# Two middle feed-forwards with one group of raw activations and an output product of seven block products

## The chip, the cores and the metric

One core of one Trainium2 chip runs the whole program. The metric is the device time of one execution in microseconds; lower is better. Before the change three executions took 1884.76, 1885.07 and 1885.96 us (median 1885.07). The engines are TensorE (PE: matmuls; its weight loads are listed apart as PEld), the vector engine (DVE), ScalarE (ACT), GpSimd (POOL, which here issues DMAs, and does so for all DMAs that add to what lies at their destination) and SyncE (SP, which issues the other DMAs). Each engine runs its own instructions strictly in the order in which they were built into the program.

## The reference

A decoder trunk of two layers on 512 tokens of width 1024. Each layer has three sub-layers: a feed-forward, a token mixer, a feed-forward. With c the conditioning vector and nine modulation vectors per layer:

```
mod = (silu(c) @ w_ada[l] + b_ada[l]).reshape(9, 1024)      # sh1, sc1, gt1, sh2, ... gt3
hn  = rms_norm(h, g_ffn1[l]) * (1 + sc1) + sh1
h   = h + 0.5 * (1 + gt1) * swiglu(hn, w_ffn1_in[l], w_ffn1_out[l])
hn  = rms_norm(h, g_mix[l]) * (1 + sc2) + sh2
h   = h + (1 + gt2) * mixer(hn)
hn  = rms_norm(h, g_ffn2[l]) * (1 + sc3) + sh3
h   = h + 0.5 * (1 + gt3) * swiglu(hn, w_ffn2_in[l], w_ffn2_out[l])

swiglu(x) = (silu(x @ w_in[:, :2816]) * (x @ w_in[:, 2816:])) @ w_out
```

So there are four feed-forwards; the middle two are the second of layer 0 and the first of layer 1. Both take their input from one norm and hand their result to the next.

## The kernel before, in words

The residual h lies in SBUF as eight tiles of 128 features by 512 tokens; "lower" and "upper" half are tokens 0 to 255 and 256 to 511 (`lo_`, `hi_`, `HALVES`). Every product is done in three matmuls: each operand is split into a high part and the remainder (`split`, L103: a cast on ACT at L104, a subtraction on DVE at L105), and high x high, high x low and low x high are summed in PSUM. A weight block of 128 x 1024 numbers is thus loaded raw (512 KB), split into `wH` and `wL` (four buffers each), and used.

A feed-forward (`ffn`) makes 22 tiles of activations, taken as 11 pairs. In the middle feed-forwards the first two pairs are products over the whole depth of 1024 (`projector`). The other nine go through `pair_in`: the pair's gate and up columns, times the two halves of depth, times the two token halves, are done as seven block products (24 matmuls of 256 columns each) instead of eight. Their weights are four raw blocks A(g, kh) and sums of them. Two sums are made by a DMA that adds at its destination (`plus`, L408, on POOL), two by DVE (L497, L524).

Before the change the middle feed-forwards work in two groups (`GROUPS`, tiles 0 to 11 and 12 to 21). The activations of a group are split at once into `actH` and `actL` (`put`); then the output product of that group runs over eight output tiles with matmuls of 512 columns (`pieces`, L93 to L95), and each tile is added to h (`residual`, L312). The last two output tiles of the second group run in token halves (`close`), so that the next norm (`norm`: `stats`, `spread`, `apply`, `low`) of the lower half goes on beside the upper half's matmuls; from there on DVE and ACT follow the order in which the code is written (`manual_schedule`).

The modulation vectors come from dots on DVE (`ada_dot`, L168): 128 rows of `w_ada`, a DMA of 512 KB from POOL's queue for each (L182), times silu(c). In the middle feed-forwards `ada_steps` puts two or three of them beside each output tile, 36 in a feed-forward.

The last feed-forward works otherwise (`whole_k`): it keeps all activations raw in one group (`raw`, six tiles), and its output product is cut in two along output features, depth and tokens and done as seven block products of 132 matmuls of 256 columns (`out_strassen`, `plan`, matmuls at L661), in 42 units whose loads, splits and sums are prepared some units ahead. Its eight dots run as half rows, one per pair (`half_dots`). Where the code sets no order, a scheduler decides it when the program is built; `issue_after` ties single instructions.

Of the kernel before, what the change touches and what calls it, by code (L numbers as in the profile page):

```python
# [8 lines left out]
F32 = mybir.dt.float32  # L9
# [7 lines left out]
P = 128  # L17
# [18 lines left out]
GROUPS = ((0, 12), (12, 22))  # L36
RWKV_WORK, ATT_WORK, FILL_WORK = 29.8, 15.2, 129.6
# [23 lines left out]
def trunk_kernel(ctx, tc, ins, out, layers=L, phases=("ffn1", "mix", "ffn2")):  # L61
# [156 lines left out]
    def norm(l, g, ish, isc, ss):  # L218
# [18 lines left out]
        def spread(sl):  # L237

            r, pt = rstd[sl.start], psum([P, T // 2], "ps_rstd", "r0" if sl.start else "x")
# [23 lines left out]
    loads = []  # L263

# [15 lines left out]
    def projector(srcs, hn, tags, pts=None, ahead=0, ready=None):  # L280
# [8 lines left out]
        if pts is None:  # L289
            pts = [psum([P, T], "ps_mm", tag) for tag in ("mm", "mm", "r1")]  # L290
            for sl in HALVES:
                for k in range(KD):
                    for w, pt in zip(ws, pts):
                        mm3(pt[:, sl], w, k, hn[k], sl, k == 0 and sl is HALVES[0], k == KD - 1 and sl is HALVES[1])
# [77 lines left out]
    def ffn(l, w_in, w_pair, w_out, hn, im, ss, need, then, ready, first=None, late=None):  # L372
# [6 lines left out]
        with tc.tile_pool(name="act", bufs=1) as ap_:  # L379
# [3 lines left out]
            whole_k = ss is None  # L383
# [26 lines left out]
            raws_ = []  # L410

            def new_raw():
                raws_.append(ap_.tile([P, 2, 2, T], F32, name="raw", tag="raw", bufs=6))
                return raws_[-1]

            def corner(X):
                return tt(X[:, 0, hi_], X[:, 1, hi_], X[:, 0, hi_], ALU.subtract)

            def new_x(p):

                if whole_k:
                    return (new_raw() if p % 2 == 0 else raws_[-1])[:, p % 2]
# [49 lines left out]
            def put(X, sl, x, y):  # L472
                if whole_k:
                    done_ = tt(X[:, :, sl], x, y, ALU.mult)
                    return corner(X) if sl is hi_ else done_
                tt(x, x, y, ALU.mult)
# [3 lines left out]
            def pair_in(p):  # L480
# [1162 lines left out]
```

## Time and profile before

| what | value |
|---|---|
| median of three executions | 1885.07 us |
| the profiled execution | 1883.92 us |
| its span, first to last instruction | 1881.8 us |
| TensorE busy | 1853.7 us (99%) |
| DVE busy | 1462.8 us (78%) |
| ACT busy | 871.5 us (46%) |
| DMA, mean over the span | 169 GB/s |
| 2nd feed-forward, from its first projection to the next one's | 621.20 to 961.02 us |
| 3rd feed-forward | 961.02 to 1301.93 us |
| last feed-forward, pairs by block products | 1595.70 to 1767.42 us |
| last feed-forward, its output product | 1767.42 to the end |

The profile is of one execution; all stage lengths below are in its time, counted from the span's first instruction. A busy share says how much of a stretch an engine had an instruction in flight. Matmuls overlap, so their rate is read from how many start in a stretch, not from the duration of one. In a row of grouped instructions the name in front is the tile that is written.

### The profile page before, as it was taken

The numbers are of one execution on the slowest core, as the hardware profiler recorded it, in microseconds if no ns is written. First come the engines' busy times: TensorE is split into PE (matmuls) and PEld (weight loads), VectorE is DVE, ScalarE is ACT, GpSimd is POOL, SyncE is SP. The second block draws the span as 40 slices with busy tenths as digits, with TensorE's granted clock in tenths as the row PEclk, the third lists the DMA queues.
The fourth block names the chain that finished last, engine by engine and source line by source line (L and its number), as shares of the span: only waits on it lengthen the run. The fifth ranks groups of instructions, "written<-read, shape, count | busy, mean of one in ns | idle before, by whom it ended". The sixth has DMA issues, their size and how long they took to land.

```text
span 1881.8 us, 37923 instructions
## 1 busy us (share of the span) xinstructions
PE 1853.7 (99%) x15796; PEld 1733.0 (92%) x15796; DVE 1462.8 (78%) x2320; ACT 871.5 (46%) x1312; POOL 155.9 (8%) x243
## 2 busy tenths in 40 slices
PE   9999999999999999999999999999999999999999
PEld 8998899897889999899899989999878889999999
DVE  7787687858886877678787776878498768888996
ACT  4453355346432555245345524544554335555653
POOL 0101100100000010110100011110000000111120
PEclk9999999999999999999999999999999999999999
DMA  8667877521222285886817688782211315787855
GB/s 305 245 180 235 261 200 235 169 71 46 75 60 71 90 228 167 291 221 188 278 56 204 174 270 234 190 267 83 91 53 60 94 39 160 213 226 210 234 129 141
DMA packets 110028, 317.19 MB, mean 169 GB/s; under 512 B 23968, under 2 KB 29088, under 8 KB 108832
## 3 DMA queue, kind: packets, MB, share of 16 engines
q1 hardware_dynamic: 78192, 203.33, 31.6%
q0 software_dynamic: 31664, 111.43, 24.2%
q8 instruction: 124, 2.03, 0.4%
q14 instruction: 48, 0.39, 0.1%
HBM read 311.31 MB, written 3.41 MB: 167 GB/s over the span
## 4 chain that ended last, share of the span: by engine, by line
PE 83%; DVE 11%; ACT 2%; issue 2%; DMA 2%; SPq 0%; ACTq 0%; DVEq 0%
PE ps_mm L101 16%; PE ps_mm L94 8%; PE ps_mm L93 8%; PE ps_mm L95 8%; PE ps_d L467 7%; PE ps_d L469 6%; PE ps_d L468 6%; PE ps_f L469 3%; PE ps_f L467 3%; PE ps_f L468 3%; PE ps_d L661 2%; PE ps_g L469 2%; PE ps_g L467 1%; PE ps_g L468 1%; PE ps_f L661 1%
## 5 line engine op out<-in xcount | busy, mean ns | idle before, releaser
L104 ACT CAST wH<-wraw 128x1024 fp32r<-128x1024 f32 (+3 forms) x266 | 249.1, 940 | 402.0 <-PE ps_mm L94 102.2
L105 DVE TENSOR_TENSOR wL<-wraw,wH 128x1024 fp32r<-128x1024 f32 (+3 forms) x266 | 286.6, 1081 | 69.2 <-ACT wH L104 68.6
L467 PE MATMUL ps_d<-comH,wH 128*128 128x256 f32 x816 | 226.1, 277 | 1.2 <-ACT s L511 0.7
L468 PE MATMUL ps_d<-comL,wH 128*128 128x256 f32 x816 | 225.3, 276 | 0.0
L469 PE MATMUL ps_d<-comH,wL 128*128 128x256 f32 x816 | 225.2, 276 | 0.0
L93 PE MATMUL ps_mm<-actH,wH 128*128 128x512 f32 (+1 forms) x588 | 216.5, 368 | 0.0
L94 PE MATMUL ps_mm<-actL,wH 128*128 128x512 f32 (+1 forms) x588 | 216.0, 367 | 0.0
L95 PE MATMUL ps_mm<-actH,wL 128*128 128x512 f32 (+1 forms) x588 | 216.0, 367 | 0.0
L168 DVE SCALAR_TENSOR_TENSOR wada<-wada,crep 128x1024 f32<-128x1024 f32 (+1 forms) x148 | 169.4, 1162 | 48.1 <-DMA wada<-in_wadaT 47.8
L101 PE MATMUL ps_mm<-hnH,wL 128*128 128x256 f32 x976 | 199.5, 282 | 1.0 <-DVE wL L105 1.0
L101 PE MATMUL ps_mm<-hnH,wH 128*128 128x256 f32 x976 | 197.4, 282 | 0.6 <-ACT wH L104 0.3
L101 PE MATMUL ps_mm<-hnL,wH 128*128 128x256 f32 x976 | 197.2, 280 | 0.0
L104 ACT CAST wH<-sum 128x1024 fp32r<-128x1024 f32 x122 | 128.5, 1054 | 139.1 <-PE ps_d L468 66.4
L105 DVE TENSOR_TENSOR wL<-sum,wH 128x1024 fp32r<-128x1024 f32 x122 | 149.1, 1223 | 54.6 <-ACT wH L104 54.5
L101 PEld LDWEIGHTS ps_mm<-hnH,wL 128*128 128x128 f32 x976 | 149.5, 188 | 8.5 <-issue 6.6
L101 PEld LDWEIGHTS ps_mm<-hnH,wH 128*128 128x128 f32 x976 | 148.7, 188 | 8.5 <-issue 5.1
L467 PEld LDWEIGHTS ps_d<-comH,wH 128*128 128x128 f32 x816 | 153.2, 188 | 2.6 <-ACT s L511 1.7
L101 PEld LDWEIGHTS ps_mm<-hnL,wH 128*128 128x128 f32 x976 | 149.5, 188 | 5.2 <-issue 4.9
L468 PEld LDWEIGHTS ps_d<-comL,wH 128*128 128x128 f32 x816 | 153.2, 188 | 0.0
L469 PEld LDWEIGHTS ps_d<-comH,wL 128*128 128x128 f32 x816 | 153.2, 188 | 0.0
L95 PEld LDWEIGHTS ps_mm<-actH,wL 128*128 128x128 f32 x588 | 110.9, 189 | 18.3
L93 PEld LDWEIGHTS ps_mm<-actH,wH 128*128 128x128 f32 x588 | 110.9, 189 | 18.2
(474 smaller groups left out, 4716.4 us busy)
## 6 DMA issues: line engine op xcount, KB each, us to landing
wada<-in_wadaT POOLq DMA_DIRECT2D x120, 512.0 KB, 5.1
wraw<-in_wmi SPq DMA_DIRECT2D x40, 512.0 KB
wraw<-in_w2p SPq DMA_DIRECT2D x36, 512.0 KB
wraw<-in_w1p SPq DMA_DIRECT2D x32, 512.0 KB
wraw<-in_w1o SPq DMA_DIRECT2D x32, 384.0 KB
wraw<-in_w1i SPq DMA_DIRECT2D x20, 512.0 KB
wraw<-in_w1o SPq DMA_DIRECT2D x32, 320.0 KB
sum<-in_w2p SPq DMA_DIRECT2D x18, 512.0 KB
```

The source lines that it names most:

```text
L93: mm(acc, wH, xH, start=start, stop=False)
L94: mm(acc, wH, xL, start=False, stop=False)
L95: mm(acc, wL, xH, start=False, stop=stop)
L101: mm(acc[:, sl], w[a][:, k], x[b][:, sl], start=start and n == 0 and sl is HALVES[0], stop=stop and n == 2, skip_group_check=True)
L104: nc.scalar.copy(hi, src)
L105: return nc.vector.tensor_sub(lo, src, hi.bitcast(F32))
L168: stt(w, w, 1.0, crep, ALU.mult, ALU.mult, accum_out=out_)
L467: mm(pt[:, i], wH, x[k][0], start=start and i + k == 0, stop=False, skip_group_check=True)
L468: mm(pt[:, i], wH, x[k][1], start=False, stop=False, skip_group_check=True)
L469: last = mm(pt[:, i], wL, x[k][0], start=False, stop=k == 3, skip_group_check=True)
L661: mm(pt[m // 2][:, m % 2], w[:, 4 * k + m], x[:, y, k], start=start and u + k + n + m % 2 == 0, stop=u == NU - 1 and n == 2, skip_group_ch ...
```

## The change

The old `ffn` stays for the first feed-forward alone and loses its `whole_k` branches. A new function `ffn_whole` serves the other three.

- Activations of all 22 tiles stay raw in six tiles R, in one group. There is no split into `actH`/`actL`, and the output stage is `out_product`: 7 block products of 132 matmuls, in 42 units, as in the last feed-forward before. Instead of writing one block product's result into two places in h, its PSUM tile pD is copied into pG by ACT, twice.
- In `pair_in` the block A(1,1) is loaded into a buffer of its own (`third` and `crep` in turn) and stays; the sum with A(1,0), made by a DMA before, is made by DVE (L735). The remaining accumulating DMA adds A(1,0) onto A(0,0) in its one buffer `first` (L746). The two last products change places.
- The dots: 36 in each middle feed-forward, by the table `DOTS` (by pair: five in each of pairs 2 to 7, three in pairs 8 and 9; none beside the output product), eight in the last (two in each of pairs 2 to 5). Their rows are loaded into parts of R that are not yet filled: three buffers up to pair 7, one from pair 8 on.
- In the middle feed-forwards the first six block products finish the upper token half of all of h; the seventh ends the lower half of output tiles 4 to 7. Beside it the next norm's upper half is written, and the next projection starts with its upper half (`lead`). The lower half's norm follows.

Line numbers of the changed kernel that matter here: split L105/L106, dot L169, dot load L700, sums L735, L745, L772, accumulating DMA L746, block product matmul L912, h L919, norm L252/L259.

```diff
+DOTS = ((0, 0, 2, 2, 2, 2), (0, 0, 5, 5, 5, 5, 5, 5, 3, 3))
...
-            for sl in HALVES:
+            first_, second_ = lead[0]
+            lead[0] = HALVES
+            for sl in (first_, second_):
...
+    def ffn_whole(l, w_in, w_pair, w_s, hn, im, ss, need, then, ready):
...
+            R = [ap_.tile([P, 2, 2, T], F32, name="raw", tag="raw", bufs=NU) for _ in range(NU)]
+            spare = [R[-2][:, 0], R[-2][:, 1], R[-1][:, 0], R[-1][:, 1]]
...
+            crow = flat(spare[3])
...
+            def dot(behind):
+                l_, i_, k = todo.pop(0)
+                w = flat(spare[turn_[0] % 3 if behind_p[0] < 8 else 2])
+                turn_[0] += 1
+                nc.gpsimd.dma_start(w, ins["wadaT"][l_, i_, k])
...
+                with queue_behind(behind):
+                    ada_dot(mod[l_, i_][:, k : k + 1], w, crow)
...
+            def pair_in(p):
...
+                S = raw(A(1, 0), ("sum0", "sum1")[p % 2], after_="a00")
+                a11 = raw(A(1, 1), ("third", "crep")[p % 2])
+                tt(S, S, a11, ALU.add)
+                with queue_behind(order["s2"] if second_ else None):
+                    S_ = hl(S)
+                prod(pF, S_, P1, True)
+                up = half_("up")
+                taken = nc.scalar.copy(up, pF)
+                a00 = raw(A(0, 0), "first", "a00")
+                prod(pD, hl(a00), B11, True)
+                s1 = half_("s1")
+                copied = nc.scalar.copy(s1, pD)
+                tt(S, S, a00, ALU.add)
+                nc.gpsimd.dma_start(a00, A(1, 0), accum_op=ALU.add)
...
+                for f in waiting:
+                    done[0] = f()
+                waiting.clear()
+                dots(done[0])
...
+                    second = hl(S)
...
+                    middle = prod(pD, second, P2, False)
...
+                    a01 = raw(A(0, 1))
+                    right = hl(a01)
+                    prod(pG, right, B21, True)
+                gate = half_("gate")
+                mark = tt(gate, pG, s1, ALU.add)
+                act(gate, gate, AF.Silu)
+                dots(mark)
+                tt(S, S, a01, ALU.add)
...
+                prod(pF, last, B22, False)
+                mark = tt(s2, pF, s2, ALU.add)
+                act(s2, s2, AF.Silu)
+                dots(mark)
+                third = hl(a00)
+                prod(pD, third, T3, False)
+                mark = tt(up, pD, up, ALU.add)
+                dots(mark)
+                tt(X[:, :, hi_], up, s2, ALU.mult)
+                mark = corner(X)
+                dots(mark)
...
+                with tc.manual_schedule(engines=HAND):
+                    for t in range(end, len(units) - 2):
+                        prepare(t)
+                        for _ in unit(t):
+                            pass
+                        if t == end:
+                            finish(5, range(4))
+                        if t == end + 1:
+                            stats(hi_)
+                            ahead(0, raws[0])
+                        if t == end + 2:
+                            spread(hi_)
+                            ahead(1, raws[1])
+                    ahead(2, raws[2])
+                    apply(hi_, range(2))
+                    k = 2
+                    for m in unit(len(units) - 1):
+                        finish(6, (m,))
+                        apply(hi_, range(k, k + 1))
+                        k += 1
+                    stats(lo_)
+                    apply(hi_, range(k, KD))
+                    ahead(3, raws[3])
+                    spread(lo_)
+                    apply(lo_, range(KD))
+                    lead[0] = (hi_, lo_)
+                    return low_()
...
-            marks = ffn(l, ins[w + "i"], ins[w + "p"], ins[w + "o"], hn, im, nss, need, then, ready, first, late)
+            if n:
+                marks = ffn_whole(l, ins[w + "i"], ins[w + "p"], ins[w + "s"], hn, im, nss, need, then, ready)
+            else:
+                marks = ffn(l, ins[w + "i"], ins[w + "p"], ins[w + "o"], hn, im, nss, need, then, ready, first, late)
```

How this moves instructions, at three places. First DVE, inside one pair of the second feed-forward. Before, one pair's middle stretch (`sum_9912` is the sum of the pair that ends, `sum_10145` that of the next):

```order
L105 TENSOR_TENSOR wL<-wraw,wH 128x1024
L478 TENSOR_TENSOR actL<-up,actH 128x2x256
L105 TENSOR_TENSOR wL<-third,wH 128x1024
L476 TENSOR_TENSOR gate<-gate,ps_d 128x512
L105 TENSOR_TENSOR wL<-sum_9912,wH 128x1024
L478 TENSOR_TENSOR actL<-gate,actH 128x2x256
L105 TENSOR_TENSOR wL<-sum_10145,wH 128x1024
L497 TENSOR_TENSOR sum_10145<-sum_10145,first 128x1024
L521 TENSOR_TENSOR gate<-ps_g,s_9975 128x512
L105 TENSOR_TENSOR wL<-first,wH 128x1024
L530 TENSOR_TENSOR up<-ps_d,up 128x512
```

The changed kernel on DVE at the like place, from the sum at L745 on (`first` is A(0,0) at the sum and has A(1,0) added when it is split further below; the dots are the rows at L169):

```order
L745 TENSOR_TENSOR sum_9218<-sum_9218,first 128x1024
L652 TENSOR_TENSOR raw<-raw 128x256
L169 SCALAR_TENSOR_TENSOR raw,mod_2_8977<-raw 128x1024
L106 TENSOR_TENSOR wL<-crep,wH 128x1024
L106 TENSOR_TENSOR wL<-sum_9218,wH 128x1024
L106 TENSOR_TENSOR wL<-wraw,wH 128x1024
L772 TENSOR_TENSOR sum_9218<-sum_9218,wraw 128x1024
L791 TENSOR_TENSOR raw<-gate,ps_d 128x2x256
L169 SCALAR_TENSOR_TENSOR raw,mod_2_8977<-raw 128x1024
L106 TENSOR_TENSOR wL<-sum_9218,wH 128x1024
L106 TENSOR_TENSOR wL<-first,wH 128x1024
L735 TENSOR_TENSOR sum_9452<-sum_9452,crep 128x1024
```

The splits of activations are gone from the pair; dots and one more sum now stand between the weight splits, and a weight split behind a dot runs after it.

Second, POOL's queue in the same feed-forward. Before, in the pairs of group 1, it holds the accumulating DMAs alone:

```order
L408 DMA third_9376<-in_w2p 128x1024
L408 DMA sum1_9446<-in_w2p 128x1024
L408 DMA third_9609<-in_w2p 128x1024
L408 DMA sum0_9679<-in_w2p 128x1024
L408 DMA third_9842<-in_w2p 128x1024
L408 DMA sum1_9912<-in_w2p 128x1024
```

The changed kernel, over two pairs (`raw_7360` and `raw_7361` are the last two tiles of R, where the dots' rows land):

```order
L746 DMA first_8305<-in_w2p 128x1024
L700 DMA raw_7360<-in_wadaT 128x1024 x2
L700 DMA raw_7361<-in_wadaT 128x1024
L700 DMA raw_7360<-in_wadaT 128x1024 x2
L746 DMA first_8541<-in_w2p 128x1024
L700 DMA raw_7361<-in_wadaT 128x1024
L700 DMA raw_7360<-in_wadaT 128x1024 x2
L700 DMA raw_7361<-in_wadaT 128x1024
L700 DMA raw_7360<-in_wadaT 128x1024
```

One accumulating DMA a pair instead of two, and five dot loads behind each.

Third, DVE where the second feed-forward hands over. Before, beside the last output tiles' upper halves, the lower half of the norm:

```order
L234 RECIPROCAL rstd<-rstd 128x2
L105 TENSOR_TENSOR wL<-wraw,wH 128x1024
L251 SCALAR_TENSOR_TENSOR hn_t<-h_86,gmod,ps_rstd 128x256
L251 SCALAR_TENSOR_TENSOR hn_t<-h_88,gmod,ps_rstd 128x256
L258 SCALAR_TENSOR_TENSOR hnL<-hn_t,mod_0_8895,hnH 128x256
L312 SCALAR_TENSOR_TENSOR h_98<-ps_mm,cg,h_98 128x256
L251 SCALAR_TENSOR_TENSOR hn_t<-h_90,gmod,ps_rstd 128x256
L258 SCALAR_TENSOR_TENSOR hnL<-hn_t,mod_0_8895,hnH 128x256
```

Changed, beside the end of the seventh block product, the upper half of the norm and the four lower tiles of h:

```order
L106 TENSOR_TENSOR wL<-wraws,wH 128x1024
L252 SCALAR_TENSOR_TENSOR hn_t<-h_86,gmod,ps_rstd 128x256
L252 SCALAR_TENSOR_TENSOR hn_t<-h_88,gmod,ps_rstd 128x256
L259 SCALAR_TENSOR_TENSOR hnL<-hn_t,mod_0_8261,hnH 128x256
L919 SCALAR_TENSOR_TENSOR h_94<-ps_g,cg,h_94 128x256
L212 TENSOR_TENSOR ss<-ss,sq 128x256
L252 SCALAR_TENSOR_TENSOR hn_t<-h_90,gmod,ps_rstd 128x256
L259 SCALAR_TENSOR_TENSOR hnL<-hn_t,mod_0_8261,hnH 128x256
L919 SCALAR_TENSOR_TENSOR h_96<-ps_g,cg,h_96 128x256
L212 TENSOR_TENSOR ss<-ss,sq 128x256
```

Four finished tiles, each with its sum of squares, alternate with rows of the norm, where before there were two.

More of the change, by code (lines that the diff above doesn't have):

```diff
@@ L237, in spread @@
         def spread(sl):
-            r, pt = rstd[sl.start], psum([P, T // 2], "ps_rstd", "r0" if sl.start else "x")
+            r, pt = rstd[sl.start], psum([P, T // 2], "ps_rstd", "r0" if sl.start and not whole_ else "x")
             for b in range(2):
@@ L428, in ffn @@
             rows_, sums = [], {}
-            free_rows = [new_raw()[:, i] for _ in range(2) for i in range(2)] if whole_k else []
-            raws_.clear()
             def whole(n):
                 for k in (2 * n, 2 * n + 4):
-                    x = free_rows.pop(0) if whole_k else ap_.tile([P, 2, T], F32, name="x", tag="act", bufs=12)
+                    x = ap_.tile([P, 2, T], F32, name="x", tag="act", bufs=12)
                     for i in range(2):
@@ L689, in ffn, with rest @@
+                tt(up, s2, up, ALU.mult)
+                put(X, hi_, up)
+                def rest():
+                    prod(pD, hl(raw(A(1, 1))), T4, False)
+                    tt(gate, pD, gate, ALU.mult)
+                    return put(X, lo_, gate)
+                waiting.append(rest)
             turn_ = [0]
@@ L702, in ffn @@
             crep = ada_crep(ap_) if n_first == 4 else None
-            sums_ = small_.tile([P, 2, KD], F32, name="adas", tag="adas", bufs=1) if whole_k else None
-            def half_dots(after):
-                l_, i_, k = todo.pop(0)
-                ws = [sp.tile([P, T], F32, name="wada", tag="ss") for _ in range(2)]
-                for n, w in enumerate(ws):
-                    nc.gpsimd.dma_start(w, ins["wadaT"][l_, i_, k, :, n * T : n * T + T])
-                with tc.issue_after(after.ins):
-                    for n, w in enumerate(ws):
-                        ada_dot(sums_[:, n, k : k + 1], w, crep[:, n * T : n * T + T])
-                if not todo:
-                    m = mod[l_, i_] = const.tile([P, KD], F32, name=f"mod{l_}_{i_}")
-                    tt(m, sums_[:, 0], sums_[:, 1], ALU.add)
-                    tt(m, m, prm(l_, "b_ada")[:, i_ * KD : i_ * KD + KD], ALU.add)
-            for g, (j0, j1) in enumerate(((0, NF),) if whole_k else GROUPS):
+            for g, (j0, j1) in enumerate(GROUPS):
                 for p in range(j0 // 2, j1 // 2):
@@ L753, in ffn @@
                         after[0] = None
-                        if whole_k and p > n_first:
-                            crep = crep or ada_crep(ap_)
-                            half_dots(done[0])
-                if whole_k:
-                    return out_strassen(waiting.pop(), raws_)
                 flush()
@@ L1369, in normed @@
         g, im = what[p]
-        return norm(l, g, im, im + 1, ss)
+        return norm(l, g, im, im + 1, ss, n > 1 and seq[n - 1][1] != "mix")
     def begin(pool):
```

458 lines of the change are left out of this document (301 added, 157 removed).

## The prediction

> **What bounds the kernel now.** I read the page first: shares of the engines, then the chain that ended last.
>
> ```profile
> span 1881.8 us, 37923 instructions
> PE 1853.7 (99%) x15796; PEld 1733.0 (92%) x15796; DVE 1462.8 (78%) x2320; ACT 871.5 (46%) x1312; POOL 155.9 (8%) x243
> PEclk9999999999999999999999999999999999999999
> PE 83%; DVE 11%; ACT 2%; issue 2%; DMA 2%; SPq 0%; ACTq 0%; DVEq 0%
> ```
>
> TensorE is the bound, at full clock. A stage is then worth its matmuls, until another engine needs more time in that stage than they do. So I cut the third sub-layer (the first of the two changed feed-forwards) into stages with the view of windows: columns are length, PE, weight loads, DVE, ACT, POOL, clock, DMA share, GB/s.
>
> ```profile
> 621.20:667.06 45.86, 45.86 (x393) 45.38 (x393) 41.86 (x70) 26.50 (x39) 1.76 (x2) 1.00 0.46 137
> 667.06:743.38 76.32, 76.32 (x675) 76.32 (x673) 58.31 (x62) 43.10 (x56) 6.77 (x9) 1.00 0.70 193
> 743.38:808.67 65.29, 65.29 (x290) 54.07 (x289) 48.34 (x81) 14.95 (x18) 12.23 (x21) 1.00 0.83 271
> 808.67:904.92 96.25, 96.09 (x841) 95.69 (x840) 72.74 (x78) 53.51 (x69) 7.70 (x10) 1.00 0.74 208
> 904.92:961.02 56.10, 56.10 (x310) 49.08 (x309) 45.17 (x81) 21.13 (x34) 6.35 (x12) 1.00 0.58 194
> 961.02:1007.96 46.94, 45.92 (x395) 45.20 (x393) 39.66 (x65) 25.12 (x36) 1.98 (x3) 1.00 0.44 127
> ```
>
> In order: two whole-depth pairs; four block-product pairs; output product of group 1; five pairs; output product of group 2 with the next norm; the same start in the next feed-forward, whose other stages have these lengths to 0.01 us. DVE has 18.0 us free of the first four pairs' 76.32 and 17 us free of the first output product, and there the modulation dots lie (three per output tile, 36 per middle feed-forward). That slack is what the change spends.
>
> **The change part by part.** *Matmuls.* The order of the changed kernel holds 2772 matmuls at L912, 3 x 7 x 132, so the saving itself is not in doubt. The last feed-forward has that stage already; two pairs and its block products, by windows:
>
> ```profile
> 864.04:883.12 19.08, 19.08 (x170) 19.08 (x169) 15.23 (x16) 11.02 (x14) 1.98 (x3) 1.00 0.63 189
> 1650.22:1669.30 19.08, 19.08 (x171) 19.08 (x170) 15.50 (x19) 9.98 (x12) 2.87 (x4) 1.00 0.79 210
> 1767.42:1782.38 14.96, 14.96 (x135) 14.96 (x134) 12.43 (x21) 7.45 (x13) 0.60 (x1) 1.00 1.02 279
> 1782.38:1798.39 16.01, 15.74 (x135) 15.54 (x133) 16.01 (x26) 10.04 (x15) 1.14 (x2) 1.00 0.30 53
> 1798.39:1815.29 16.90, 15.89 (x135) 15.49 (x133) 16.54 (x26) 9.39 (x13) 0.86 (x1) 1.00 0.36 110
> 1815.29:1861.93 46.64, 46.64 (x399) 46.64 (x397) 38.22 (x60) 26.23 (x41) 13.81 (x16) 1.00 0.92 209
> ```
>
> A pair takes 19.08 us and a block product of 132 matmuls 14.96 at its best (113.3 ns each). Before, pairs and output of a middle feed-forward last 76.32 + 65.29 + 96.25 + 56.10 = 293.96 us; after, 9 x 19.08 + 7 x 14.96 = 276.44. **-17.5 each, -35.0 for both.**
>
> *What the block products really take.* The second to sixth in the rows last 16.01 + 16.90 + 46.64 = 79.55 instead of 74.80: waits for split weights, and behind each wait TensorE goes on at 117.8 ns (46.64 us for 396) with nothing waited for. With the seventh at that rate (+0.6) this is +5.3 per feed-forward; bounds 0 (no wait) and 12 (six products like the 16.90 one). I take +5.3, since the changed stage has the same matmuls, splits and order of blocks: **+10.7 for both** (0 to 24).
>
> *Vector engine in the pairs.* Durations overlap, so I count start to start, from the timeline of DVE:
>
> ```profile
> 778.04 1.22 DVE L168 SCALAR_TENSOR_TENSOR wada<-wada,crep 128x1024 f32<-128x1024 f32 x1
> 779.19 0.08 DVE L168 DVE_READ_ACCUMULATOR wada<-wada,crep 128x1 f32 x1
> ...
> 847.28 0.68 DVE L476 TENSOR_TENSOR up<-up,s 128x512 f32<-128x512 f32 x1
> 847.88 1.22 DVE L524 TENSOR_TENSOR sum<-sum,wraw 128x1024 f32<-128x1024 f32 x1
> 849.02 1.22 DVE L105 TENSOR_TENSOR wL<-wraw,wH 128x1024 fp32r<-128x1024 f32 x1
> 850.15 0.68 DVE L478 TENSOR_TENSOR actL<-up,actH 128x512 fp32r<-128x512 f32 x1
> ```
>
> and two grouped rows (mean duration behind the comma), the corner and ACT's cast of a weight block:
>
> ```profile
> L417 DVE TENSOR_TENSOR raw<-raw 128x256 f32<-128x256 f32 x11 | 4.6, 418 | 0.0
> ...
> L104 ACT CAST wH<-first 128x1024 fp32r<-128x1024 f32 x34 | 35.8, 1053 | 43.6 <-PE ps_g L468 23.7 <-DMA first<-in_w1p 9.6 <-DMA first<-in_w2p 7.4
> ```
>
> So 1.14 us for 1024 columns, 0.60 for 512, 1.15 for a dot. A pair before: 7 weight splits and 2 sums (9 x 1.14) and 7 half-size operations (4.20) = 14.5 us. After: one sum more on DVE instead of on a DMA (10 x 1.14 = 11.40), 5 half-size (3.00), a corner (about 0.34: its 0.42, less the 0.08 by which the others overlap) = 14.74, and in six pairs five dots (5.75): **20.49 us against TensorE's 19.08**. DVE's stream alone costs 1.41 us in each of these pairs; that is the floor of the loss, 8.5 per feed-forward. In the two pairs with three dots it is 18.19, in the last 14.74.
>
> *What DVE waits for.* The accumulating DMA onto `first` is issued behind the sum at L745, and the five dot loads stand behind it in POOL's queue. Sizes and medians from issue to landing, and POOL's own timeline:
>
> ```profile
> wada<-in_wadaT POOLq DMA_DIRECT2D x120, 512.0 KB, 5.1
> sum<-in_w2p POOLq DMA_DIRECT2D x18, 512.0 KB, 7.8
> third<-in_w2p POOLq DMA_DIRECT2D x18, 512.0 KB, 6.6
> third<-in_w1p POOLq DMA_DIRECT2D x16, 512.0 KB, 5.9
> ...
> 1643.77 0.87 POOL L408 DMA_DIRECT2D third<-in_w2p  x1 [2.07 <-ACT s L511]
> 1644.31 0.90 POOL L709 DMA_DIRECT2D wada<-in_wadaT  x1
> ```
>
> The accumulate lands 5.9 to 7.8 us after its issue. I take 5.9, since it now has the accumulating queue to itself. The first dot's 512 KB follow it: 1.9 us at the 271 GB/s of the window above. So the dot's data are there 7.8 us after L745. DVE's program has 0.34 + 1.15 + 4 x 1.14 + 0.60 = 6.65 us between (in the first order of the changed kernel, above): it waits 1.2 us (0 if the accumulate took 4.7 or less; 3.1 at 7.8), and the weight split behind the dot waits with it.
>
> A second loop: `first` is one buffer, reloaded on SP behind the split at its use as third block, and the sum and load of the next pair stand behind that issue. Between the two splits DVE has 2 x 1.14 + 2 x 1.15 + 2 x 0.60 = 5.78 us. Reload 5.1 (the plain load's median is the nearest row) and 1.05 for the cast make 6.15: 0.4 more (0 to 3). A pair of five dots: 20.49 + 1.2 + 0.4 = 22.1, **+3.0**. At the start of the six DVE runs ahead of TensorE by a few splits; half of one pair's loss I count as absorbed. In the two pairs with three dots one buffer serves all, so each dot waits for a 5.1 us reload with some 4.1 us of work between: 18.19 + 1.2 + 2 x 1.1 = 21.6, +2.5 each. Per feed-forward 5.5 x 3.0 + 2 x 2.5 = 21.5: **+43.0 for both** (floor 17; with the 7.8 us accumulate in all eight pairs 21.5 + 8 x 1.9 = 36.7 each, 73).
>
> Could the loads be the bound themselves? A five-dot pair moves ten blocks of 512 KB, 5.2 MB. At 271 GB/s they need 19.3 us, at the 210 GB/s of a pair with accumulates 25.
>
> By the Trainium skill ("DMA: Bandwidth & Descriptors", the section on the anatomy of a DMA from GpSimd) such a DMA takes 2.0 us and its bytes at 436 GB/s, so 3.2 us for 512 KB. The 5.1 above disagrees. By the page neither dot nor reload would be waited for, which is the first rival below.
>
> *The hand-over.* The seventh product runs beside the next norm's upper half. Upper rows cost DVE two operations of about 0.40 each, and a finished tile 0.40 and 0.34 (the means below, less the overlap of 0.08):
>
> ```profile
> L251 DVE SCALAR_TENSOR_TENSOR hn_t<-h,gmod,ps_rstd 128x256 f32<-128x256 f32 x80 | 37.4, 473 | 0.0
> L258 DVE SCALAR_TENSOR_TENSOR hnL<-hn_t,mod,hnH 128x256 fp32r<-128x256 f32 x80 | 38.2, 478 | 0.9 <-ACT hnH L252 0.9
> L668 DVE SCALAR_TENSOR_TENSOR h<-ps_g,cg,h 128x256 f32<-128x256 f32 x8 | 3.7, 478 | 8.3 <-PE ps_g L661 8.3
> L340 DVE TENSOR_TENSOR ss<-ss,sq 128x256 f32<-128x256 f32 x20 | 8.4, 421 | 4.4 <-ACT sq L215 4.2
> ```
>
> After the first of four tiles (3.1 us before the product ends) that is 4 x 0.74 + 6 x 0.80 = 7.8 us, so 4.7 us after its end; the projection needs its last upper rows 7 x 9 matmuls, 7.1 us, after it. The lower half (8 x 0.80) then follows in step. DVE may reach this late by two of its weight splits. The start stages above take 45.86 and 46.94 us for 384 matmuls (43.5 at 113.3 ns), so 2.4 to 3.4 of stall is paid now as well. I take **0** (-2 to +4 each).
>
> *Last feed-forward.* Two dots in its pairs 2 to 5 instead of one half-pair of loads in all nine: the accumulate loop is 7.8 + 11.5 us of DVE work = 19.3, +0.3 a pair; output stage alike: **+1** (-3 to +4). The removed split of activations (ACT and DVE, in the pairs) and the weight order of pF and pD were hidden under matmuls and save nothing.
>
> Sum: -35.0 + 10.7 + 43.0 + 0 + 1.0 = **+19.7 us** on the profiled execution's 1883.92 us (span 1881.8 and 2.1 around it); that lies 1.15 under the median of 1885.07, so about 1905 there.
>
> **The rivals.** *Faster: DVE's stream alone sets the pace.* If dots and reload always land in time, the pairs lose 17 instead of 43, and the sum is -6 us: 1879. It decides at a five-dot pair below some 20.6 us (with the three-dot pairs' loss halved as well, 12 x 1.5 + 5 = 23 us, what the rest of the sum gains). For it: the plain load is 5.1 with neighbours. Against: the dot stands behind an accumulate of 5.9 or more. 18%; another 6% that even DVE's excess is absorbed (-23, 1862), against which stands 20.49 > 19.08.
>
> *DMA paces the pairs.* At 210 GB/s a pair takes 25 us, 12 x 5.9 + 10 = 81 instead of 43: 1943. For it: the DMA share of 0.79 with one half of these dots; against: 0.83 at 271 GB/s. 10%.
>
> *The clock.* TensorE now pauses some 3 us in a pair; before, its clock shows full throughout. If a pause halved it for 3 us after, each costs 1.5: +18, 1923. 3%. By the Trainium skill ("TensorE: Matmul & The Clock Gate", Part 1) an idle window of about 3.4 us halves the clock; no run here shows it yet.
>
> *It balances.* Block products without waits (-10.7) and a dot that waits half as long (12 x 0.6 less) leave +2, within a measurement of 1885. 8%.
>
> **How the numbers follow.** My forecast, slower by waits of DVE in the pairs: 55% (1890 to 1928). A measurement here tells about 0.2%, 3.8 us, from no change. Faster: 18 + 6 = 24%; same 8%; slower the rest, 68%. The range leaves out the 6% at the bottom and the DMA rival's upper half, and reaches 1872 to 1936.
>
> **What would show it.** Pairs 3 to 7 of the middle feed-forwards at 21 to 23 us, DVE busy in over 19.5 of it, dots (L169) waiting for their load, TensorE waiting for wL; the last pair near 19.1; block products 15 to 17 us. Wrong if those pairs stand at 19.1 to 20.6, or at 24 and more with the DMA share near 1; or if the loss is in the block products or behind the seventh.

## The result, and the profile after

The changed kernel takes 1930.27 us (median of four, 1928.44 to 1943.29) against 1885.51 us before: ratio 1.0248, 95% interval 1.0201 to 1.0295. The forecast was 1905. The sign was right; the loss is 44.8 us where 20 were forecast. The profiled execution took 1931.10 us, 47.2 more than that of before. Its page:

```profile
span 1929.3 us, 39531 instructions
PE 1856.3 (96%) x16468; PEld 1760.8 (91%) x16468; DVE 1571.6 (81%) x2483; ACT 923.3 (48%) x1416; POOL 167.6 (9%) x254
PE 56%; DVE 25%; DMA 9%; issue 5%; ACT 4%; SPq 1%; POOL 0%; ACTq 0%; DVEq 0%; POOLq 0%
```

TensorE's share of the chain that ended last fell from 83% to 56%; DVE's rose from 11% to 25%, and DMA's from 2% to 9%. The matmuls were saved, and TensorE waits instead. Where, the view of windows tells: pairs 2 to 9 of the second feed-forward, its last pair with the transition to the output product, the first six block products, the seventh with the next start, and the nine pairs of the last feed-forward (columns as in the prediction):

```profile
669.92:837.33 167.41, 159.38 (x1346) 156.29 (x1345) 157.46 (x204) 77.77 (x97) 24.09 (x40) 0.99 0.70 220
837.33:862.46 25.13, 22.86 (x178) 22.41 (x177) 24.04 (x36) 13.16 (x21) 4.15 (x5) 0.93 0.88 248
862.46:954.14 91.68, 89.53 (x787) 89.10 (x785) 79.90 (x124) 56.45 (x90) 16.55 (x20) 1.00 0.70 171
954.14:1027.59 73.45, 65.89 (x534) 63.86 (x533) 59.15 (x97) 36.30 (x55) 3.06 (x5) 0.98 0.38 130
1632.46:1815.06 182.60, 177.01 (x1524) 175.69 (x1522) 149.59 (x176) 91.47 (x116) 13.16 (x17) 0.99 0.52 153
```

Against TensorE's own time (19.08 a pair, 113.3 ns a matmul; the start at the 46.94 of before), in us:

| term | forecast, each | 2nd feed-forward | 3rd | last |
|---|---|---|---|---|
| matmuls saved | -17.5 | -17.5 | -17.5 | |
| pairs 2 to 9 | +21.5 | +14.8 | +18.9 | |
| last pair, transition | 0 | +5.1 | +5.2 | |
| six block products | +5.3 with the seventh | +2.8 | +0.1 | |
| seventh, next start | 0 | +11.6 | +10.4 (the remainder) | |
| sum | +9.3 | +16.8 | +17.1 | +10.7, of it 9.9 in the pairs (forecast +1) |

The sums and 2.9 us ahead of the first block-product pair make the 47.5 us between the spans. Of those 2.9, 2.0 lie ahead of the second feed-forward (its first projection starts at 623.15 us, before at 621.20), in unchanged work: from 10 to 30 us the granted clock was 0.66 here and 0.91 in the trace of before, and kernels below with the same start show values from the one to the other. The other 0.9 lie in the two whole-depth pairs.

The prediction's mechanism in the pairs was dots that wait for their loads. DVE's waits in pairs 3 to 9 of the second feed-forward (total, times, longest) say otherwise; the dots waited once:

```profile
DVE wL L106 <- ACT wH L105: 3.1, 3, 1.2
DVE raw L169 <- DMA raw<-in_wadaT: 1.8, 1, 1.8
DVE sum L735 <- DMA third<-in_w2p: 1.4, 1, 1.4
```

A usual pair of five dots, the longest one, and a pair of three dots:

```profile
752.64:772.72 20.08, 19.66 (x171) 19.27 (x169) 20.08 (x25) 9.79 (x12) 3.53 (x6) 1.00 0.81 259
708.99:732.01 23.02, 21.23 (x170) 20.85 (x169) 21.89 (x29) 9.77 (x12) 3.58 (x7) 0.93 0.76 239
815.23:837.33 22.10, 20.00 (x170) 19.41 (x169) 19.74 (x29) 10.35 (x14) 2.49 (x4) 1.00 0.55 167
```

Pairs 3 to 7 lasted 19.99, 23.02, 20.63, 20.08 and 20.54 us, pairs 8 and 9 with three dots 21.97 and 22.10. In the third feed-forward it is 20.06 to 20.67 with one of 24.21, then 23.90 and 22.47. So eight of ten five-dot pairs stand at DVE's own 20.49, where the prediction had 22.1, and the pairs with fewer dots are longer than most with five.

### The profile page after: what moved, and what is told of

Read it like the earlier page. It is cut to its first block, busy times and chain, and to the rows that moved or that the text cites. A ratio compares the mean times of both kernels' runs of the same rounds, so it can differ in the third digit from the quotient of the medians.

```text
span 1929.3 us, 39531 instructions
## 1 busy us (share of the span) xinstructions
PE 1856.3 (96%) x16468; PEld 1760.8 (91%) x16468; DVE 1571.6 (81%) x2483; ACT 923.3 (48%) x1416; POOL 167.6 (9%) x254
## 3 DMA queue, kind: packets, MB, share of 16 engines
HBM read 300.30 MB, written 3.41 MB: 157 GB/s over the span
## 4 chain that ended last, share of the span: by engine, by line
PE 56%; DVE 25%; DMA 9%; issue 5%; ACT 4%; SPq 1%; POOL 0%; ACTq 0%; DVEq 0%; POOLq 0%
PE ps_mm L102 15%; DVE wL L106 7%; PE ps_d L912 5%; PE ps_mm L95 3%; PE ps_mm L94 3%; PE ps_mm L96 3%; PE ps_f L912 3%; PE ps_g L912 3%; ACT wH L105 2%; DMA first<-in_w2p 2%; PE ps_d L687 2%; DVE raw L169 2%; PE ps_d L689 2%; PE ps_d L688 2%; DMA rowk<-in_w2s 1%
## 5 line engine op out<-in xcount | busy, mean ns | idle before, releaser
L105 ACT CAST wH<-wraw 128x1024 fp32r<-128x1024 f32 (+2 forms) x183 | 178.4, 977 | 244.0 <-PE ps_mm L102 68.1
L105 ACT CAST wH<-sum 128x1024 fp32r<-128x1024 f32 x159 | 167.1, 1051 | 187.0 <-DVE sum L772 68.7
L106 DVE TENSOR_TENSOR wL<-wraw,wH 128x1024 fp32r<-128x1024 f32 (+2 forms) x183 | 206.1, 1128 | 51.8 <-ACT wH L105 51.5
L106 DVE TENSOR_TENSOR wL<-sum,wH 128x1024 fp32r<-128x1024 f32 x159 | 194.1, 1221 | 24.6 <-ACT wH L105 24.4
L688 PE MATMUL ps_d<-comL,wH 128*128 128x256 f32 x648 | 183.1, 283 | 0.0
L912 PE MATMUL ps_d<-xs,wH 128*128 128x256 f32 x792 | 136.0, 277 | 0.0
L912 PEld LDWEIGHTS ps_d<-xs,wH 128*128 128x128 f32 x792 | 119.5, 188 | 0.0
L912 PE MATMUL ps_d<-xs,wL 128*128 128x256 f32 x396 | 109.7, 277 | 1.6 <-DVE wL L106 1.6
L169 DVE SCALAR_TENSOR_TENSOR raw<-raw 128x1024 f32<-128x1024 f32 x80 | 97.4, 1218 | 10.7 <-ACT raw L1027 8.0
L105 ACT CAST wH<-first 128x1024 fp32r<-128x1024 f32 x61 | 64.2, 1052 | 82.3 <-DMA first<-in_w2p 48.0
L700 POOL DMA_DIRECT2D raw<-in_wadaT x80 | 42.9, 537 | 636.7 <-DVE q L674 331.3
```

The costliest lines, as they stand in the source:

```text
L105: nc.scalar.copy(hi, src)
L106: return nc.vector.tensor_sub(lo, src, hi.bitcast(F32))
L169: stt(w, w, 1.0, crep, ALU.mult, ALU.mult, accum_out=out_)
L688: mm(pt[:, i], wH, x[k][1], start=False, stop=False, skip_group_check=True)
L700: nc.gpsimd.dma_start(w, ins["wadaT"][l_, i_, k])
L912: mm(pt[m // 2][:, m % 2], w[:, 4 * k + m], x[:, y, k], start=start and u + k + n + m % 2 == 0, stop=u == NU - 1 and n == 2, skip_group_ch ...
```

## The experiments

Theories: *length* (DVE's stream in a pair with dots is longer than TensorE's, loads or not); *load* (what the queues bring is late); and, from the last feed-forward's trace, *loop* (the one buffer `first`, below).

### The dots and their loads apart

**Neither dots nor loads.**

```diff
-                w = flat(spare[turn_[0] % 3 if behind_p[0] < 8 else 2])
-                turn_[0] += 1
-                nc.gpsimd.dma_start(w, ins["wadaT"][l_, i_, k])
...
+                    nc.vector.memset(mod[l_, i_], 0.0)
+                return
...
```

> Leaves out the 80 dots of the three changed feed-forwards and their loads; those modulation vectors are zero. Length theory (DVE has more work in a pair with dots than TensorE, so the pairs run at DVE's pace, loads or no loads): the eight dot pairs of a middle feed-forward go from 167.4 and 171.5 us to 153 to 156, the last pair with the transition from 25.1 to 20 to 22, the last feed-forward's pairs back to 19.1 each, the hand-over stays; in all 1880 to 1888 us. Load theory (the prediction: dots and sums wait for what the GpSimd queue brings): the same number here. A third, that the new sum L735 waits for its block A(1,1) whatever the dots do: pairs stay at 20 us and more, last feed-forward too, 1905 us or more.

Measured 1882.33 us, ratio 0.9975 (0.9962 to 0.9989). Pairs 2 to 9, last pair with transition, seventh with the next start, and the last feed-forward's pairs:

```profile
669.08:822.18 153.10, 153.01 (x1346) 152.79 (x1345) 117.73 (x126) 78.60 (x96) 6.85 (x8) 1.00 0.44 129
822.18:842.34 20.16, 20.16 (x178) 20.08 (x177) 19.97 (x30) 12.98 (x20) 3.42 (x4) 1.00 0.93 270
934.31:1008.15 73.84, 66.53 (x535) 64.82 (x533) 58.21 (x97) 36.25 (x55) 0.86 (x1) 0.95 0.33 107
1591.67:1765.08 173.41, 173.04 (x1524) 172.84 (x1523) 139.50 (x156) 92.32 (x116) 10.25 (x12) 1.00 0.50 147
```

All pairs stand at TensorE's rate, so without dots and their loads nothing is lost there, in the last feed-forward either; the new sum alone costs nothing. The hand-over keeps its 73.8 us: it has nothing to do with the dots. With the block products it eats nearly all of the saving: even without 80 dots the kernel is only 0.25% faster than before.

**Dots without loads.**

```diff
-                nc.gpsimd.dma_start(w, ins["wadaT"][l_, i_, k])
...
-                    ada_dot(mod[l_, i_][:, k : k + 1], w, crow)
+                    stt(w, crow, 1.0, crow, ALU.mult, ALU.mult, accum_out=mod[l_, i_][:, k : k + 1])
```

> The 80 dots run on DVE, but over the silu(c) tile alone (both inputs), so that nothing is loaded for them and the modulation vectors hold other numbers. Length theory: 1918 to 1932, pairs with five dots still 20 to 22 us. Load theory: the waits go, five-dot pairs 19.1 to 20.5 us, 1885 to 1900.

Measured 1910.61 us, between the two. Pairs 2 to 9, one five-dot pair, and the last feed-forward's pairs:

```profile
667.73:829.48 161.75, 156.81 (x1346) 154.33 (x1345) 154.11 (x203) 78.25 (x96) 5.99 (x7) 1.00 0.41 121
727.30:747.70 20.40, 19.62 (x171) 19.24 (x170) 20.40 (x28) 9.77 (x12) 0.85 (x1) 1.00 0.43 130
1612.81:1795.15 182.34, 176.21 (x1523) 175.31 (x1522) 146.70 (x174) 91.78 (x116) 10.28 (x12) 0.99 0.48 141
```

In the five-dot pair DVE is busy for all of 20.40 us, the 20.49 that the prediction summed. That floor is real: 9.1 us over TensorE's 152.64 in these pairs, of the changed kernel's 14.8. The other 5.7 go with the loads. In the last feed-forward the loads explain nothing (182.34 here, 182.60 with them).

**Loads without dots.**

```diff
                 nc.gpsimd.dma_start(w, ins["wadaT"][l_, i_, k])
...
-                begun.setdefault((l_, i_), k)
...
+                return
```

> The 80 loads stay, the 80 dots on DVE are left out (those modulation vectors are zero). Length theory: within 6 us of the kernel without both, 1880 to 1892. Load theory: the queue and the memory traffic are as in the changed kernel, accumulated block and reloads come as late as there, so most of the loss stays: 1905 to 1925.

Measured 1937.80 us, above both numbers. This does not decide: with no dot to wait for, up to fourteen loads stand in a row behind one accumulating DMA in the GpSimd queue, where the changed kernel has five, and the slow pairs (up to 31.9 us) come with the bursts.

**Loads at the changed kernel's pace, dots over 64 columns.**

```diff
-                    ada_dot(mod[l_, i_][:, k : k + 1], w, crow)
+                    ada_dot(mod[l_, i_][:, k : k + 1], w[:, :64], crow[:, :64])
```

> All 80 loads stay, and each load waits for the dot before it, but a dot runs over 64 of the 1024 columns only (the modulation vectors hold other numbers). So the loads keep the changed kernel's pace (where dots are left out altogether, nine to eleven loads follow one another in the GpSimd queue) and DVE's time for the dots is gone. Length theory: DVE's time was the cost, 1882 to 1895 us. Load theory: the loads delay the accumulated block and the reloads by themselves, 1908 to 1925 us.

Measured 1916.40 us (1910.93 to 1925.02; the profile is of the slowest execution): the load theory's number. Pairs 2 to 9, then DVE's waits in pairs 3 to 7:

```profile
673.33:840.48 167.15, 157.36 (x1347) 155.90 (x1345) 125.02 (x204) 77.61 (x96) 25.02 (x41) 0.99 0.66 218
```

```profile
DVE sum L745 <- DMA first<-in_w2p: 17.4, 5, 4.6
DVE sum L735 <- DMA third<-in_w2p: 6.0, 3, 2.9
DVE sum L735 <- DMA crep<-in_w2p: 3.6, 2, 1.9
```

DVE has 42 us of idle time here and the pairs are as long as with full dots (167.15 to 167.41). What is late is not a dot but the reload of `first`. From issue to ACT's cast it takes 4.3 to 5.7 us here against 3.3 to 3.9 in the kernel without the dot loads, and the accumulating DMA lands 5.9 us after its issue in the median against 5.2. So the pairs have two limits of nearly one height, DVE's stream and the loop through `first` with the dots' traffic beside it. They don't add up: each alone gives most of the 14.8 us, and taking one away wins only a part, 5.7 us without the loads and 0.3 with short dots.

### The loop through `first`

Pair 5 of the last feed-forward in the changed kernel, timeline of DVE, POOL, SP and ACT (start, duration, instruction, idle time before it and what ended it):

```profile
1689.88 1.05 ACT L105 CAST wH<-first 128x1024 fp32r<-128x1024 f32 x1 [6.37 <-DMA first<-in_w2p]
...
1692.71 1.22 DVE L745 TENSOR_TENSOR sum<-sum,first 128x1024 f32<-128x1024 f32 x1
1694.47 0.87 POOL L746 DMA_DIRECT2D first<-in_w2p  x1 [9.23 <-DVE sum L745]
...
1701.79 1.05 ACT L105 CAST wH<-first 128x1024 fp32r<-128x1024 f32 x1 [1.07 <-DMA first<-in_w2p]
1701.99 1.23 DVE L735 TENSOR_TENSOR sum<-sum,third 128x1024 f32<-128x1024 f32 x1 [1.78 <-DMA third<-in_w2p]
...
1704.86 1.22 DVE L169 SCALAR_TENSOR_TENSOR raw<-raw 128x1024 f32<-128x1024 f32 x1
...
1706.01 1.22 DVE L106 TENSOR_TENSOR wL<-first,wH 128x1024 fp32r<-128x1024 f32 x1
1707.25 0.33 SPq L648 DMA_DIRECT2D first<-in_w2p  x1
...
1711.06 1.05 ACT L105 CAST wH<-first 128x1024 fp32r<-128x1024 f32 x1 [4.21 <-DMA first<-in_w2p]
```

Cast to cast over one turn is 21.18 us: split and sum 4.6, accumulating DMA 7.3, split 5.5, reload 3.8. The second split could start at 1702.84 and starts 3.2 us later, because L735, waiting 1.78 us for A(1,1), a split, a product and a dot stand ahead of it in DVE's order. In the kernel without dots and loads the turns took 17.7 to 20.3 us (18.5 from 721.00 to 739.52), about the length of a pair, with waits for TensorE in most of them; so at most 1.4 us is seen to be free in a pair of 19.08.

**A second buffer in pairs 3, 5 and 7.**

```diff
-                a00 = raw(A(0, 0), "first", "a00")
+                a00 = raw(A(0, 0), "first", "a00", None, flat(spare[2]).rearrange("p (k c) -> p k c", c=P) if p in (3, 5, 7) else None)
...
-                w = flat(spare[turn_[0] % 3 if behind_p[0] < 8 else 2])
+                w = flat(spare[turn_[0] % 2 if behind_p[0] < 8 else 2])
```

> The changed kernel with a second buffer for A(0,0): in pairs 3, 5 and 7 it is loaded, added to and split in the sixth tile's first half of R; the dots use two buffers instead of three up to pair 7. Loop theory (one buffer is loaded, split, summed, added to by the accumulating DMA, split again and only then reloaded: 4.3 + 2.8 + 1.2 + 7.9 + 2.3 = 18.5 us without any wait on DVE, so that whatever stands in DVE's order between these steps, two dots for instance, lengthens the pair): the last feed-forward's pairs 4 to 7, now 22.1, 23.4, 20.1 and 19.8 us, go to 19.1 to 19.5, and the middle ones lose the share of the loads, five-dot pairs 20.0 to 20.6 us; 1908 to 1918 us. Rival (it is the new sum's wait for A(1,1), or DVE's order, that holds those pairs): the last feed-forward within 2 us of the changed kernel, 1925 to 1932 us in all.

Measured 1912.84 us. Pairs 2 to 9 of the second feed-forward, and all pairs of the last:

```profile
667.13:833.55 166.42, 158.72 (x1347) 156.42 (x1345) 156.32 (x203) 76.77 (x95) 24.66 (x41) 0.99 0.67 220
1624.59:1797.98 173.39, 173.03 (x1524) 172.83 (x1522) 150.08 (x175) 92.89 (x116) 13.94 (x18) 1.00 0.53 161
```

In the last feed-forward the loss is gone with all dots in place (182.60 to 173.39): there the loop was the cause. In the middle ones nearly all of it stays. DVE's stream, the other limit, gives 161.75 of the 166.42 us (the kernel without loads); which wait makes the other 4.7 is not shown.

**The sum with A(1,1) by DMA again.**

```diff
-                tt(S, S, a11, ALU.add)
+                nc.gpsimd.dma_start(S, A(1, 1), accum_op=ALU.add)
```

> Undoes one part of the change: the sum of A(1,0) and A(1,1) is made by an accumulating DMA again, not by DVE at L735; A(1,1) is also still loaded into its own buffer. A pair has 1.14 us less on DVE, one block of 512 KB and one accumulating DMA more. Length theory: five-dot pairs 19.35 to 20 us, 1905 to 1915 us in all. Load theory: the second accumulating DMA comes ahead of the first in the GpSimd queue, pairs no shorter, 1928 to 1945 us.

Measured 1924.47 us, neither number. The last feed-forward's pairs fall to 174.59 us, since L735 and its wait no longer stand in the loop; pairs 2 to 9 of the second feed-forward stay at 166.61 with DVE 13.4 us less busy (144.09). So here lowering DVE's stream alone wins next to nothing; that the other limit held the pairs is argued from this, not shown.

**Dots spread over pairs 2 to 10, with and without that sum on DVE** (both with the second buffer and the late third block of the next part).

```diff
-DOTS = ((0, 0, 2, 2, 2, 2), (0, 0, 5, 5, 5, 5, 5, 5, 3, 3))
+DOTS = ((0, 0, 2, 2, 2, 2), (0, 0, 5, 5, 4, 4, 4, 4, 4, 4, 2))
```

> The changed kernel with the second buffer for A(0,0) in pairs 3, 5 and 7, the third weight block of the hand-over split behind the norm's first two rows, and the 36 dots spread as 5, 5, 4, 4, 4, 4, 4, 4, 2 over pairs 2 to 10. DVE's stream of the nine pairs is then 9 x 14.74 + 36 x 1.15 = 174.1 us as before, but no run of six pairs is over TensorE's 171.7 by more than 2.4. Two-limits theory (a pair takes the longer of DVE's stream and the loop of the A(0,0) buffer): the pairs and the transition cost 4 to 8 us a middle feed-forward over TensorE's own time, where they cost 20 and 24; with the last feed-forward's 9.9 and 2 to each hand-over, 1885 to 1895 us in all. If the loads themselves are the limit (memory traffic): 1903 to 1913, no better than the second buffer alone.

> The kernel with second buffer, late third block and evenly spread dots, and the sum with A(1,1) made by an accumulating DMA again. DVE's stream of nine pairs is 163.8 us, under TensorE's 171.7, and a pair moves 10 to 11 blocks of 512 KB, 275 to 302 GB/s at TensorE's pace. Two-limits theory: 1876 to 1886 us, the pairs within 3 us of TensorE's own time. Load theory (traffic and the GpSimd queue, in which two accumulating DMAs and four dot loads follow one another): 1900 us or more, pairs over 20 us with DVE idle in more than 2 us of each.

Measured 1934.58 and 1950.94 us: the first kernel misses both theories' numbers, the second has the load theory's. Pairs 2 to 9 and the last pair with transition of the first kernel, pairs 2 to 9 of the second, and the first one's DVE waits from 800 us, in pair 8, to the end of the transition:

```profile
666.84:833.26 166.42, 158.18 (x1346) 155.47 (x1345) 150.38 (x191) 75.39 (x94) 23.07 (x38) 1.00 0.64 207
833.26:871.21 37.95, 25.28 (x179) 23.98 (x180) 27.48 (x42) 14.88 (x23) 6.03 (x8) 0.87 0.88 259
671.76:844.93 173.17, 160.43 (x1346) 158.01 (x1345) 142.05 (x183) 75.87 (x94) 28.24 (x44) 0.98 0.74 225
```

```profile
DVE raw L169 <- DMA raw<-in_wadaT: 12.8, 4, 4.4
```

From pair 8 on one tile of R is left for the dots, so each waits for its own load, the activations of pair 10 go into the same tile, and the output product's first loads begin there. With the sum by DMA, the accumulating DMAs come on top. In that second kernel both limits are lowered, DVE idles 31 us in pairs 2 to 9, and they still take 173.17: so the two limits are not the whole account of the middle pairs. DVE waits 9.5 us for the dots' loads there from 665 to 800 us, the kind of wait that the prediction had expected; how much of it is the GpSimd queue and how much memory traffic, no run separates.

**Six dots in pairs 2 to 7, none later** (again with the second buffer and the late third block).

```diff
-DOTS = ((0, 0, 2, 2, 2, 2), (0, 0, 5, 5, 5, 5, 5, 5, 3, 3))
+DOTS = ((0, 0, 2, 2, 2, 2), (0, 0, 6, 6, 6, 6, 6, 6))
...
-                dots(done[0])
+                dots(done[0], 1 + (len(share) > 6))
```

> The second buffer for A(0,0), the late third block, and all 36 dots in pairs 2 to 7, six in each with two buffers, none in pairs 8 to 10, where only one buffer is left for them. Theory that the one buffer costs the last pairs: pairs 3 to 7 at DVE's 14.74 + 6 x 1.15 = 21.6 us, pairs 8 and 9 at 19.1, the last pair with the transition at 20 to 21, so 12 to 15 us over TensorE's time where the second buffer alone has 18 and 20: 1894 to 1902 us. Rival (eleven blocks a pair are too much for the queues, or DVE's lag stays to the end): pairs 3 to 7 at 22.5 us and more or the last ones over 20, 1905 to 1920 us.

Measured 1929.30 us, above both numbers. Pairs 2 to 8, then pairs 9 and 10 with the transition, and the dots' waits:

```profile
667.07:827.20 160.13, 143.42 (x1178) 139.03 (x1177) 145.03 (x192) 68.23 (x84) 24.57 (x41) 0.99 0.66 214
827.20:866.42 39.22, 39.22 (x346) 39.14 (x345) 35.62 (x47) 22.83 (x32) 4.30 (x5) 1.00 0.70 203
```

```profile
DVE raw L169 <- DMA raw<-in_wadaT: 7.4, 7, 2.0
```

Half of the theory held: without late dots the last pair and the transition cost nothing (39.22 us, against 39.1 for 345 matmuls at 113.3 ns). But with six loads a pair through two buffers a six-dot pair lasts 24 us, where DVE needs 21.6. Why the four-dot pairs of the evenly spread kernel (19.3 us of DVE each) stayed at 20.0 to 21.3 in the second feed-forward is not settled.

### The hand-over

The longest waits from 954 to 984 us in the changed kernel, and the stall in the view of windows:

```profile
ACT wH L105 <- DMA wraws<-in_w1i: 4.0, 1, 4.0
DVE wL L106 <- ACT wH L105: 3.9, 3, 3.2
...
PE ps_mm L94 <- ACT hnH L253: 3.4, 1, 3.4
```

```profile
970.42:974.12 3.70, 0.28 (x3) 0.07 (x1) 2.02 (x4) 1.60 (x3) 0.00 (x0) 1.00 0.59 238
974.12:978.20 4.08, 4.08 (x20) 3.97 (x21) 2.50 (x6) 1.27 (x3) 0.00 (x0) 0.58 0.00 0
961.79:1027.59 65.80, 59.51 (x486) 57.94 (x485) 53.66 (x87) 32.37 (x48) 3.06 (x5) 0.97 0.42 145
```

The next projection's third weight block is loaded into a tile of R that only the last units set free. ACT waits for it, the norm's first upper row stands behind that, and TensorE behind the row, then at a clock of 0.58. The third row is the stretch that the next kernels change.

**TensorE's order: the seventh product first.**

```diff
-                        mm3(pt[:, sl], w, k, hn[k], sl, k == 0 and sl is first_, k == KD - 1 and sl is second_)
+                        with behind_all([m for m in out_last if m]): mm3(pt[:, sl], w, k, hn[k], sl, k == 0 and sl is first_, k == KD - 1 and sl is second_)
```

> The changed kernel with TensorE's order at the hand-over changed: the next projection's first matmuls (seven between two groups of the seventh product, eighteen before its last group) are held until the product's last matmul. Order theory (18 ready matmuls stand behind seven that wait 3.7 us for the norm's first upper row, and the wait then halves the clock for 3.4 us): 2 us of matmuls fill the wait, no half clock there, so 3 to 4 us less in each hand-over, 1922 to 1925 us. Rival (DVE's rows of the norm set the end of the hand-over; the matmuls are only done earlier and TensorE waits later): 1927 to 1931 us, the start of the next feed-forward as much longer.

**The third block's split behind the first two rows.**

```diff
-                    ahead(2, raws[2])
                     apply(hi_, range(2))
+                    ahead(2, raws[2])
```

> The changed kernel with two lines of the hand-over swapped: the third weight block of the next projection (its load lands in a tile of R, 5.7 us after issue) is split behind the norm's first two upper rows, not ahead of them. In the changed kernel ACT's cast of that block waits 4.0 us for the load, DVE's split for the cast, and the first rows of the norm stand behind both; TensorE then waits 3.7 us for the first row and goes on at half clock for 3.4 us. Wait theory: both go, 4 to 6 us less in each hand-over, 1918 to 1923 us. Rival (the third block is needed just as early, the wait only moves to TensorE's first matmuls with it; or h and the norm's rows set the end anyway): 1926 to 1931 us.

**The same, with the upper rows' subtraction done twice.**

```diff
+            twice[0] and sl.start and stt(hn[i][1][:, sl], t, sh, hn[i][0][:, sl].bitcast(F32), ALU.add, ALU.subtract)
             return a, stt(hn[i][1][:, sl], t, sh, hn[i][0][:, sl].bitcast(F32), ALU.add, ALU.subtract)
...
```

> The kernel with the late third block (1925.15 us), and each of the eight upper rows' subtractions at the hand-over is done twice on DVE (the second writes the same numbers): 8 x 0.40 = 3.2 us of DVE work more in each hand-over. If DVE's stream sets the length of the hand-over: 2.4 to 3.2 us more in each, from the first lower tile's group to the next first block-product pair 67 to 68 us instead of 64.5 in the second feed-forward, 1930 to 1932 us. If TensorE's order, ACT or the loads set it: within 1 us each, 1924 to 1927.

Measured 1933.40, 1925.15 and 1935.68 us. The same stretch in each, in this order:

```profile
960.54:1028.50 67.96, 59.49 (x486) 58.59 (x485) 53.81 (x87) 32.53 (x48) 3.07 (x5) 0.92 0.41 142
```

```profile
958.55:1023.09 64.54, 59.78 (x487) 58.00 (x485) 53.64 (x87) 32.37 (x48) 3.07 (x5) 0.97 0.43 149
```

```profile
967.00:1035.02 68.02, 61.85 (x486) 59.90 (x485) 57.50 (x95) 32.38 (x48) 3.05 (x5) 0.95 0.41 144
```

TensorE's order was not the cause: with the product first it waits 7.6 us for DVE's tiles of h (L919) and runs longer at half clock, 2.2 us more in all. Taking the load's wait from ahead of the rows gives 1.3 us here (2.2 with the mixer behind the third feed-forward), not 4 to 6. And 3.2 us more DVE work make the stretch 3.5 us longer (64.54 to 68.02), part of it at half clock; TensorE's waits for the rows doubled (L260 there) come to 4.8 us. That profile is of the slowest of four executions, 1924 to 1940 us, so the total is too wide to tell. It fits DVE's stream as what sets the hand-over: finished tiles, sums of squares, rows of the norm and splits of weights and activations alternate on it, with waits for ACT and TensorE in between. It is not shown for the rows done once, and how the remaining 10 us divide is open.

## Why the prediction was wrong

- *Matmuls, -35*: right; the kernel without dots shows the pairs at 19.08.
- *Block products, +10.7*: mis-sized. The first six cost 2.9 in both feed-forwards; five of the third's ran at 113.3 ns.
- *DVE's stream, 20.49 a pair*: right to 0.1 us (20.40, DVE busy throughout).
- *The dot behind the accumulating DMA, +1.2 a pair*: this step failed. Dots waited 1.8 us in seven pairs, and eight of ten five-dot pairs lasted 19.99 to 20.67 us, where the prediction said that 19.1 to 20.6 would show it wrong. The accumulating DMA's price was nearly right (below, 5.4 and 5.6 us median against 5.9), but the prediction priced it and the reload as two loops, each against the DVE work beside it. They are one loop through one buffer, whose turn is about as long as a pair.
- *Pairs, +43.0*: 44.0 measured, with 10.3 of it in the last pair and transition, counted at 0 (with no dots behind pair 7 that part goes, 39.22 above). The five-dot pairs lost less than their 3.0 each, 2.0 in the mean over pairs 3 to 7, the three-dot pairs more than their 2.5, 3.5 in the mean. The sum agreed by luck, not by its parts.
- *Last feed-forward, +1*: 10.7. The same loop. The prediction set 7.8 us of DMA and 11.5 of DVE work against the pair, +0.3 each, and left the reload out; how little room the whole turn has went unseen.
- *The hand-over, 0*: 22.0 for both, the largest miss. The step summed 7.8 us of DVE work behind the product's first tile and did not ask when the next projection's third block has a buffer, nor what the waits between DVE's tiles, rows and splits cost. The first of these was worth 1.3 and 2.2 us; the rest stays open.
- *The clock rival, 3%*: in part. Eight half-clock stretches of 3.41 us lie in the changed feed-forwards, none there before (the one before lies at the program's start, so its clock was not full throughout); at 1.7 us each that is up to 13.6 us, where TensorE would not have waited anyhow.
- *The DMA rival, 10%*: not so here. The changed pairs run at a DMA share of 0.66 and 220 GB/s, and those of five dots last 21.0 in the mean over pairs 3 to 7, not 25.

The rival of DVE's stream alone (1879) is what most five-dot pairs show. Its nearest run as a whole is the kernel without loads, 1910.6: the hand-over and the last feed-forward's loop were in neither sum. The issue rows of the changed kernel, median from issue to landing behind the last comma:

```profile
raw<-in_wadaT POOLq DMA_DIRECT2D x80, 512.0 KB, 4.5
...
first<-in_w2p POOLq DMA_DIRECT2D x18, 512.0 KB, 5.4
...
first<-in_w1p POOLq DMA_DIRECT2D x9, 512.0 KB, 5.6
```

By the Trainium skill ("DMA: Bandwidth & Descriptors", the anatomy of a DMA from GpSimd) 512 KB would be there 3.2 us after issue, an estimate from its fixed time and rate; the dot loads' row says 4.5.

None of the kernels that compute all dots beats the one before.

## What to carry to other kernels

Follow a single buffer once round, through every DMA, split and sum until it is loaded again, and compare that turn with the stage: DVE work off the bound still lengthens it wherever it stands in the strict order between two steps. Slack in an engine's busy time is not room: on DVE nine pairs had 39 us of it (19.08 less 14.74 each) for 41 us of dots, 2 too few, and pairs with the transition lost 20, as loads, buffers and order decided. Where two limits lie at one height, taking one away shows little; test each with the other one gone, and where both are gone and the time stays, look for a third.

## What the runs showed of the hardware

The granted clock falls in fixed stretches. All eight half-clock stretches of the changed feed-forwards are 3.41 us long and start at whole multiples of 3.413 us from one another (715.32, 858.68, 974.74, 1114.68, ..., 1701.78). The stretch ahead of the first of them, that one, and two others that were not followed by half clock:

```profile
711.91:715.32 3.41, 1.62 (x12) 1.24 (x11) 3.41 (x5) 2.44 (x3) 1.43 (x2) 1.00 0.78 187
715.32:718.73 3.41, 3.41 (x18) 3.41 (x17) 2.49 (x3) 0.83 (x1) 0.00 (x0) 0.50 1.02 292
947.43:950.84 3.41, 1.78 (x15) 1.55 (x14) 3.41 (x7) 2.69 (x5) 0.00 (x0) 1.00 0.01 3
1186.36:1189.77 3.41, 1.60 (x15) 1.40 (x13) 2.87 (x3) 1.53 (x2) 0.00 (x0) 1.00 0.04 17
```

PE busy for 1.62 of 3.41 us was followed by half clock, 1.78 was not, and neither was 1.60, so the edge is not at one share. Over the thirteen traces of the changed kernel and the kernels above, every full-clock stretch of this grid with 1.96 us idle or more was followed by half clock; of those with 1.43 to 1.91 some were and some were not. The place counts too: a pause of 1.78 us inside one stretch (712.14 to 713.92) cost half clock, one of 3.10 us split over two (1187.96 to 1191.06) did not. By the Trainium skill ("TensorE: Matmul & The Clock Gate", Part 1) the window is 3413 ns and free-running, and an idle window halves the clock; the trace agrees with the grid, but here 1.96 us of idle time in a window were enough.
